# K, V and the first Q tiles from weighted but unnormalised input, with the root mean square applied at the PSUM exit

## The chip, the cores and the metric

The kernel runs as one program on all 8 cores of a Trainium2 chip; each core handles its own tokens and no core waits for another. The metric is device time in microseconds (us) of the slowest core. A program on all eight cores falls into a slower state in some executions: the cores of one die, or of both, show a lower granted TensorE clock (the share of its full speed that the chip allows it), and the run takes some per cent longer.

The engines are named as the profile names them: PE (TensorE), PEld (its weight loads), DVE (VectorE), ACT (ScalarE), POOL (GpSimd) and SP (SyncE, here an issuer of transfers). A `q` after a name (SPq) is the engine's queue, where it issues DMAs.

## The reference

One layer of a decoder: an RMS norm, a wide projection, two branches (sliding-window attention and a gated convolution), gates, and an MLP. Only the first step matters here.

```python
def _rmsnorm(x, g):
    y = x * lax.rsqrt(jnp.mean(x * x, axis=-1, keepdims=True) + EPS)
    return y * g

n = _rmsnorm(hp, norm1_g[l])                 # D_MODEL = 2048
q, k, v, u, g = _project(n, w_in[l], ...)    # one matmul, its columns split
ya = _prompt_attention(q, k, v, sink[l])     # scores, exp, values
# ... u goes through a depthwise convolution of width 31; gates, w_out, MLP follow
```

The root mean square is one number per token, and the projection is linear. So `rmsnorm(x) @ W` equals `(x * g) @ W`, scaled per token afterwards. K, V and Q can therefore be multiplied before the sum of squares is known. The change is built on this.

## The kernel before

Tokens lie on the free axis, features on the 128 partitions in 16 tiles (`XF[...][:, k, :]`). The first group has 768 tokens, processed as three chunks of 256. Each weight "slab" is 2 MB of f32 in DRAM, loaded through GpSimd's queue and converted to bf16 on the way. There are five slots. In the code, `mm` is a chain of matmuls into one PSUM bank, `act` is a ScalarE activation, `tt` and `stt` are VectorE operations on two tensors (`stt` with a per-partition scalar in between), and `P.dma(..., after=[...])` adds a wait for whatever last wrote the tiles that are named.

```python
def first_norm(c):                              # chunk c of the first group
    cc = slice(256 * c, 256 * c + 256)
    pairs = []
    for q in range(4):                          # four quarters of the 16 feature tiles
        t = tI[q]
        act(t[:, :, :], xs[c][:, 4 * q:4 * q + 4, :], AF.Square)
        tt(t[:, 0:2, :], t[:, 0:2, :], t[:, 2:4, :], ALU.add)
        pairs += [(onesf[:, :], t[:, k, :]) for k in range(2)]
    b = bank()
    mm(b[:, 0:256], pairs)                      # 8 f32 matmuls with ones / D
    act(R1[:, cc], b[:, 0:256], AF.Sqrt, bias=EPS)
    P.op("dve", "reciprocal", out=R1[:, cc], in_=R1[:, cc])
    for k in range(16):                         # the 16 scalings
        stt(XF[0][:, k, cc], xs[c][:, k, :], v1(V_G1 + k), R1[:, cc], ALU.mult, ALU.mult)

load_slab(after=[xs[0][:, 0, :]])               # loads are paced: x, slab, x, slab, ...
first_load(1, [wsl[0][:, :]])
load_slab(after=[xs[1][:, 0, :]])
first_load(2, [xs[1][:, 12, :]])
# ... [cut: three more slabs]
first_norm(0)

# ... [cut] in the first group's front:
wk = slab()
keys(wk, 0, 256)                                # K of chunk 0: 2 x 16 matmuls, evicted by ScalarE
first_norm(1)
keys(wk, 256, 256)
wv = slab(load=False)
for t in range(4):
    vals(wv, t)                                 # V of four 128-token tiles
first_norm(2)
load_slab()
keys(wk, 512, 256)
vals(wv, 4)
vals(wv, 5)
load_slab()
constants()
```

`constants` ends with eight products that spread the convolution's taps into small diagonal blocks, and a store of the result to DRAM, from where it is reloaded later in another layout:

```python
for m in range(8):
    P.op("dve", "tensor_tensor", out=cwst[:, m, :, :],
         in0=ctap[:, 32 * m:32 * m + 32].unsqueeze(2).broadcast_to([128, 32, 32]),
         in1=ctap[:, 256:288].unsqueeze(1).broadcast_to([128, 32, 32]), op=ALU.mult)
P.dma("sp", cwb[:, :, :], cwst[...], "d_cwb")
```

After that comes Q (eight tiles of 16 matmuls in each of two column chunks, `128x320` in the trace), and then blocks of attention between the last Q tiles: scores, `exp` into eight probability tiles `PT` (the `exp` also is the PSUM eviction), then the values matmul.

The softmax here doesn't subtract the row's maximum and nothing guards it: scores larger than these inputs give would overflow.

## Time and profile before

| | before |
|---|---|
| time | 3396.55 us median of 3 runs (3395.22 to 3692.71; the highest is a slow run) |
| span of the profiled cores | 3373.6 to 3390.5 us, all fast |
| first K matmul | 19.5 us |
| third chunk's K done | 75.9 us |
| first Q matmul | 79.3 us |
| first scores matmul | 98.9 us |
| first `exp` | 99.5 us |
| first values matmul | 104.4 us |

The last six rows are medians of the eight cores, from the timeline. They serve as milestones throughout.

The page of the kernel before, lines of its parts 1, 2 and 4. Part 2 cuts the span into 40 slices and gives the busy tenths of PE and the granted clock in tenths; part 4 is the chain of work that ended last. In this and all later views, lines in between are left out.

```profile
span 3390.5 us, 59039 instructions; the slowest of 8 cores (3373.6 to 3390.5 us)
PE   6979999999999999999999999999999999999998
PEclk7989999999999999999999999999999999999999
PE 94%; DMA 2%; DVE 2%; SPq 1%; issue 1%; ACT 0%; DVEq 0%; ACTq 0%; POOLq 0%
```

PE is busy 9 tenths or more nearly everywhere. What is left to gain lies in the first slices of about 85 us each, so the most this change could touch is some tens of us in 3390. The start is read from core 1. Its timeline before: start us, duration us, engine, line (one helper records every operation, so all have one line), operation, output<-inputs, shape, count, and in brackets the idle time before it with what ended it.

```profile
18.25 6.42 DVE L157 SCALAR_TENSOR_TENSOR XF_79<-xs_105,vec,R_58 128x256 bf16<-128x256 f32 x16 [0.17 <-DVE R_58 L157]
20.00 8.34 PE L157 MATMUL ps<-XF_79,wsl_49 128*128 128x256 bf16 x32 [4.26 <-DVE XF_79 L157]
66.73 9.38 PE L157 MATMUL ps<-XF_79,wsl_49 128*128 128x256 bf16 x32 [3.17 <-DVE XF_79 L157]
79.44 8.86 PE L157 MATMUL ps<-XF_79,wsl_51 128*128 128x320 bf16 x64
82.71 9.17 DVE L157 TENSOR_TENSOR cwst<-ctap 128x1024 bf16<-128x1024 f32 x8
91.95 0.33 SPq L157 DMA_DIRECT2D cwb<-cwst  x1
99.09 0.61 PE L157 MATMUL ps<-XQ_84,kT 64*128 64x512 bf16 x4
```

Sixteen scalings take 6.42 us, 0.40 us each, and the first sixteen K matmuls of a chunk follow them one by one; the 32 of a chunk take 8.3 to 9.6 us. The Q matmuls in the same list take 0.14 us each, although they are wider. The eight tap products are 1.15 us each on DVE, and the store of their result is issued at 91.95 us.

Where PE waited in the first 110 us of core 1 before (from the waits of PE: total us, times, longest), and its busy time in two stretches (columns: PE, PEld, DVE, ACT and POOL busy, granted clock, DMA share, GB/s):

```profile
PE ps L157 <- DVE tI_101 L157: 12.0, 2, 9.6
PE ps L157 <- DVE XF_79 L157: 10.5, 3, 4.3
PE ps L157 <- ACT tI_102 L157: 2.5, 1, 2.5
```

```profile
0.00:80.00 80.00, 53.41 (x245) 33.91 (x246) 33.41 (x67) 18.95 (x29) 3.50 (x10) 0.81 0.69 151
80.00:110.00 30.00, 30.00 (x222) 20.28 (x219) 13.88 (x14) 10.91 (x23) 6.92 (x12) 1.00 1.01 198
```

The waits are for sums of squares (`tI`) and for scaled input (`XF`). The longest, 9.6 us, is the one from the start of the span to the first sums. The mean clock in the first 80 us reads 0.81. That is too high, since the view counts all time before its first record of the clock as full speed: four matmuls of the sums took 2.05 us at 9.61 us on core 1, and 1.03 us at 14.72 us. The Trainium skill (TensorE: Matmul & The Clock Gate, "Part 1: The HAM clock gate") says that the clock gate passes half the pulses until PE has been busy for some microseconds. The trace agrees in the stretches where scalings pace K: the windows table of core 4 shows a clock of 0.50 from 20 to 25 us and from 40 to 45 us. From 80 to 110 us PE is never idle, at full clock.

### The profile page before, as it was taken

Reading aid. Unit: us, or ns where it says so; the run is one execution under the profiler, and the core shown is the slowest. Engines: PE = TensorE matmul, PEld = TensorE weight load, DVE = VectorE, ACT = ScalarE, POOL = GpSimd, SP = SyncE. Lnnn points to the kernel's source line nnn. Section 1 sums busy time; section 2 is a strip of 40 time slices with the busy share of each in tenths; the row PEclk is TensorE's granted clock in tenths of the full one; section 3 lists DMA queues with packets and bytes.
Section 4 is the critical chain, followed back from the end, with each engine's and each line's share of the span. In section 5 each row is a group of like instructions: output and inputs, shape, how many; then the busy total and the mean of one; then the engine's idle time right before and its main releaser. Section 6 shows DMA issues by size and latency. Waiting matters only on the chain.

```text
span 3390.5 us, 59039 instructions; the slowest of 8 cores (3373.6 to 3390.5 us)
## 1 busy us (share of the span) xinstructions
PE 3312.6 (98%) x22688; PEld 2161.1 (64%) x22688; DVE 1621.9 (48%) x2438; ACT 718.6 (21%) x1371; POOL 267.9 (8%) x475
## 2 busy tenths in 40 slices
PE   6979999999999999999999999999999999999998
PEld 4556776567777775666655666666666666666667
DVE  4534333668889453225288666644542232222225
ACT  2323223321211222112242020203211230101022
POOL 0200000300000000000130000000000000000000
PEclk7989999999999999999999999999999999999999
DMA  6766997467776696858648655555778656668651
GB/s 150 143 119 135 194 188 153 84 123 140 139 142 119 118 197 141 191 110 177 123 83 158 114 102 104 104 102 112 156 165 194 111 110 112 112 109 150 109 106 70
DMA packets 88770, 446.79 MB, mean 132 GB/s; under 512 B 11024, under 2 KB 19920, under 8 KB 45648
## 3 DMA queue, kind: packets, MB, share of 16 engines
q0 software_dynamic: 48240, 349.36, 57.3%
q1 hardware_dynamic: 39968, 93.12, 9.1%
q8 instruction: 187, 3.06, 0.4%
q14 instruction: 87, 0.71, 0.1%
q10 hardware_dynamic: 288, 0.52, 0.0%
HBM read 766.65 MB, written 25.94 MB: 234 GB/s over the span
## 4 chain that ended last, share of the span: by engine, by line
PE 94%; DMA 2%; DVE 2%; SPq 1%; issue 1%; ACT 0%; DVEq 0%; ACTq 0%; POOLq 0%
PE ps L157 94%; SPq L157 1%; DMA ush_89<-um_95 1%; DVE rden_68 L157 0%; DMA wsl_49<-wst 0%; DVE rden_67 L157 0%; DVE H L157 0%; DMA xs_106<-xp 0%; DMA xrP_121<-x 0%; DMA xs_107<-xp 0%; DMA xs_105<-xp 0%; DMA ush_88<-um_94 0%; ACT TQ L157 0%; DVE XF_79 L157 0%; DVE XQ_84 L157 0%
## 5 line engine op out<-in xcount | busy, mean ns | idle before, releaser
L157 DVE TENSOR_TENSOR H<-ps,H 128x320 f32<-128x320 f32 (+4 forms) x400 | 202.7, 507 | 378.1 <-PE ps L157 377.9
L157 PE MATMUL ps<-XF_79,wsl_49 128*128 128x320 bf16 (+3 forms) x1568 | 243.2, 312 | 11.8 <-DVE XF_79 L157 6.3
L157 PE MATMUL ps<-XF_79,wsl_53 128*128 128x320 bf16 (+2 forms) x1472 | 219.6, 309 | 0.0
L157 PE MATMUL ps<-XF_79,wsl_52 128*128 128x320 bf16 (+2 forms) x1472 | 219.4, 310 | 0.0
L157 PE MATMUL ps<-XF_79,wsl_50 128*128 128x320 bf16 (+2 forms) x1472 | 217.7, 308 | 0.8 <-DVE XF_79 L157 0.5
L157 PEld LDWEIGHTS ps<-XF_79,wsl_49 128*128 128x128 bf16 x1568 | 155.1, 99 | 97.0 <-issue 26.4
L157 PE MATMUL ps<-XF_81,wsl_49 128*128 128x384 bf16 (+2 forms) x1344 | 210.2, 317 | 0.0
L157 PE MATMUL ps<-XF_81,wsl_52 128*128 128x384 bf16 (+2 forms) x1344 | 206.0, 314 | 0.0
L157 PE MATMUL ps<-XF_81,wsl_50 128*128 128x384 bf16 (+2 forms) x1280 | 200.0, 317 | 0.0
L157 PE MATMUL ps<-XF_79,wsl_51 128*128 128x320 bf16 (+2 forms) x1344 | 197.8, 307 | 0.0
L157 PE MATMUL ps<-XF_81,wsl_53 128*128 128x384 bf16 (+2 forms) x1280 | 197.4, 315 | 0.0
L157 PEld LDWEIGHTS ps<-XF_79,wsl_53 128*128 128x128 bf16 x1472 | 143.5, 98 | 73.0 <-issue 2.7
L157 PEld LDWEIGHTS ps<-XF_79,wsl_52 128*128 128x128 bf16 x1472 | 143.7, 98 | 72.1 <-issue 1.4
L157 PEld LDWEIGHTS ps<-XF_79,wsl_50 128*128 128x128 bf16 x1472 | 143.4, 98 | 71.7 <-issue 4.0
L157 PE MATMUL ps<-XF_81,wsl_51 128*128 128x384 bf16 (+2 forms) x1216 | 186.5, 314 | 0.0
L157 PEld LDWEIGHTS ps<-XF_81,wsl_49 128*128 128x128 bf16 x1344 | 132.0, 98 | 74.6 <-issue 0.4
L157 DVE SCALAR_TENSOR_TENSOR tAP<-tAP,ps 128x384 f32<-128x384 f32 (+1 forms) x64 | 34.4, 537 | 302.5 <-PE ps L157 301.6
L157 PE MATMUL ps<-XF_80,wsl_49 128*128 128x352 bf16 (+4 forms) x1184 | 178.8, 311 | 0.0
L157 PEld LDWEIGHTS ps<-XF_81,wsl_52 128*128 128x128 bf16 x1344 | 131.3, 98 | 71.3 <-issue 1.0
L157 PEld LDWEIGHTS ps<-XF_79,wsl_51 128*128 128x128 bf16 x1344 | 131.1, 98 | 63.7 <-issue 2.1
L157 PEld LDWEIGHTS ps<-XF_81,wsl_50 128*128 128x128 bf16 x1280 | 125.6, 98 | 71.3 <-issue 1.4
L157 PE MATMUL ps<-XF_80,wsl_51 128*128 128x352 bf16 (+4 forms) x1120 | 170.6, 313 | 0.0
(406 smaller groups left out, 4575.5 us busy)
## 6 DMA issues: line engine op xcount, KB each, us to landing
wsl_49<-wst POOLq DMA_DIRECT2D x66, 1024.0 KB, 8.2
wsl_50<-wst POOLq DMA_DIRECT2D x66, 1024.0 KB, 8.3
wsl_51<-wst POOLq DMA_DIRECT2D x65, 1024.0 KB, 8.3
wsl_52<-wst POOLq DMA_DIRECT2D x65, 1024.0 KB, 8.2
wsl_53<-wst POOLq DMA_DIRECT2D x65, 1024.0 KB, 8.1
xrP_121<-x SPq DMA_DIRECT2D x18, 384.0 KB, 7.6
xrP_123<-x SPq DMA_DIRECT2D x18, 352.0 KB, 5.4
H<-x SPq DMA_DIRECT2D x16, 384.0 KB, 10.2
```

The source lines that it names most:

```text
L157: i = getattr(eng, ins[0])(**ins[1])
```

## The change

Its intent: K, V and four Q tiles (two of the eight in the code's count, each in two column chunks) read `x * g`, which needs no root mean square; the results are scaled as they leave PSUM, where an eviction is needed anyway. The squares are added on GpSimd, which has nothing to do at that time, and PE sums four tiles instead of eight. All of x is loaded at once, without pacing. The tap products move to GpSimd and into the memory of the probability tiles, because their old place is now the weighted input's.

```diff
-        cwst = over(X[1], 0, "cwst", [128, 8, 32, 32], BF16)
-        ctap = over(X[1], 16384, "ctap", [128, 288], F32)
+        cwst = over(PT[0], 0, "cwst", [128, 8, 32, 32], BF16)
+        ctap = over(X[2], 16384, "ctap", [128, 288], F32)
# ... [cut]
+        P.dma("act", vec[:, :], vecs[:, :], "d_vec")
+        for c in range(3):
+            first_load(c)                       # no after=
+        def squares(c, q):
+            t = tI[q]
+            act(t[:, :, :], xs[c][:, 4 * q:4 * q + 4, :], AF.Square)
+            for k in (2, 1):
+                P.op("pool", "tensor_tensor", out=t[:, 0:k, :], in0=t[:, 0:k, :], in1=t[:, k:2 * k, :], op=ALU.add)
+        def weigh(c, q):                        # XF[1] = x * g, one op of 128x1024 per quarter
+            ...
+        def first_rstd(c):
+            mm(b[:, 0:256], [(onesf[:, :], tI[q][:, 0, :]) for q in range(4)])
+            ...                                 # Sqrt, reciprocal as before
# ... [cut] constants():
-                P.op("dve", "tensor_tensor", out=cwst[:, m, :, :],
+                P.op("pool", "tensor_tensor", out=cwst[:, m, :, :],
# ... [cut] front of the first group:
+                first_keys(0)                   # evicted by VectorE, times R1
+                for q in range(4):
+                    first_scale(0, q)           # 4 of the old 16 scalings, for the later projections
+                    squares(1, q)
+                    weigh(1, q)
+                first_rstd(1)
+                first_keys(1)
+                for t in range(4):
+                    first_vals(t)               # evicted by ScalarE with a per-token scale
+                for q in range(4):
+                    first_scale(1, q)
+                    squares(2, q)
+                    weigh(2, q)
+                    if q < 2:
+                        load_slab(after=[xs[2][:, 4 + 8 * q, :]])
+                first_rstd(2)
+                first_keys(2)
+                first_vals(4)
+                first_vals(5)
+                load_slab()
+                load_slab()
+                for q in range(4):
+                    first_scale(2, q)
+                constants()
# ... [cut] Q:
-                    b = fm(w, j % 2, nT, halo + c0, n)
-                    act(qo[:, j, c0:c0 + n], b[:, 0:n], AF.Copy)
+                    b = fm(w, j % 2, XF[1] if first and j < 2 else nT, halo + c0, n)
+                    if first and j < 2:
+                        tt(qo[:, j, c0:c0 + n], b[:, 0:n], R1[:, halo + c0:halo + c0 + n], ALU.mult)
+                    else:
+                        act(qo[:, j, c0:c0 + n], b[:, 0:n], AF.Copy)
```

The third Q tile and everything after it still read scaled input, so the 48 scalings remain; they only move later.

More of the change, by code (lines that the diff above doesn't have):

```diff
@@ L359, in drain, with first_load @@
                 side.pop(0)()
-        for q in range(4):
-            P.dma("sp", xs[0][:, 4 * q:4 * q + 4, :], xp[0][:, 4 * q:4 * q + 4, :], f"d_x{q}")
-        P.dma("sp", vec[:, :], vecs[:, :], "d_vec")
+        def first_load(c):
+            for q in range(4):
+                P.dma("sp", xs[c][:, 4 * q:4 * q + 4, :], xp[c][:, 4 * q:4 * q + 4, :], f"d_x{q}")
+        P.dma("act", vec[:, :], vecs[:, :], "d_vec")
+        for c in range(3):
+            first_load(c)
         P.dma("sp", ctap[:, :], cwd[:, :], "d_ct")
@@ L383, in add_square @@
                 tt(dst[:, c0:c0 + n], dst[:, c0:c0 + n], t, ALU.add)
-        def first_norm(c):
-            cc = slice(256 * c, 256 * c + 256)
-            pairs = []
-            for q in range(4):
-                t = tI[q]
-                act(t[:, :, :], xs[c][:, 4 * q:4 * q + 4, :], AF.Square)
-                tt(t[:, 0:2, :], t[:, 0:2, :], t[:, 2:4, :], ALU.add)
-                pairs += [(onesf[:, :], t[:, k, :]) for k in range(2)]
+        one = S1[0:1, 0:1]
+        P.op("dve", "memset", ap=one, constant=1.0)
@@ new lines, in squares @@
+        def squares(c, q):
[4 more added lines that the diff above has]
+        def weigh(c, q):
+            f = slice(4 * q, 4 * q + 4)
+            P.op("dve", "tensor_tensor", out=XF[1][:, f, 256 * c:256 * c + 256], in0=xs[c][:, f, :],
+                 in1=vec[:, V_G1 + 4 * q:V_G1 + 4 * q + 4].unsqueeze(2).broadcast_to([128, 4, 256]), op=ALU.mult)
@@ L394, in first_norm, with first_scale @@
+        def first_rstd(c):
+            cc = slice(256 * c, 256 * c + 256)
             b = bank()
-            mm(b[:, 0:256], pairs)
+            mm(b[:, 0:256], [(onesf[:, :], tI[q][:, 0, :]) for q in range(4)])
             act(R1[:, cc], b[:, 0:256], AF.Sqrt, bias=EPS)
             P.op("dve", "reciprocal", out=R1[:, cc], in_=R1[:, cc])
-            for k in range(16):
+        def first_scale(c, q):
+            cc = slice(256 * c, 256 * c + 256)
+            for k in range(4 * q, 4 * q + 4):
@@ L399, in first_norm @@
                 stt(XF[0][:, k, cc], xs[c][:, k, :], v1(V_G1 + k), R1[:, cc], ALU.mult, ALU.mult)
-        def first_load(c, after):
-            for q in range(4):
-                P.dma("sp", xs[c][:, 4 * q:4 * q + 4, :], xp[c][:, 4 * q:4 * q + 4, :], f"d_x{q}", after=after)
-        load_slab(after=[xs[0][:, 0, :]])
-        first_load(1, [wsl[0][:, :]])
-        load_slab(after=[xs[1][:, 0, :]])
-        first_load(2, [xs[1][:, 12, :]])
-        load_slab(after=[xs[2][:, 0, :]])
-        load_slab()
@@ L411, in build, with first_column @@
-        first_norm(0)
+        def first_column(t):
+            b = bank()
+            mm(b[:, 0:1], [(R1[0:1, 128 * t:128 * t + 128], one)])
+            act(S2[:, t:t + 1], b[:, 0:1], AF.Copy)
+        load_slab()
+        for q in range(4):
+            squares(0, q)
+            weigh(0, q)
+        load_slab(after=[xs[1][:, 4, :]])
+        first_rstd(0)
         def constants():
@@ L652, in front, with first_keys, first_vals @@
             if first:
-                wk = slab()
-                keys(wk, 0, 256)
-                first_norm(1)
-                keys(wk, 256, 256)
-                wv = slab(load=False)
-                for t in range(4):
-                    vals(wv, t)
-                first_norm(2)
+                wk, wv = slab(), slab(load=False)
+                def first_keys(c):
+                    cc = slice(256 * c, 256 * c + 256)
+                    for a in range(2):
+                        b = fm(wk, a, XF[1], 256 * c, 256)
+                        tt(kT[:, a, cc], b[:, 0:256], R1[:, cc], ALU.mult)
+                def first_vals(t):
+                    first_column(t)
+                    b = bank()
+                    mm(b[:, 0:256], [(XF[1][:, k, 128 * t:128 * t + 128], wv[:, k, :]) for k in range(16)])
+                    act(vtok[:, t, :], b[:, 0:256], AF.Copy, scale=S2[:, t:t + 1])
+                first_keys(0)
[5 more added lines that the diff above has]
+                first_keys(1)
+                for t in range(4):
+                    first_vals(t)
+                for q in range(4):
+                    first_scale(1, q)
[7 more added lines that the diff above has]
+                first_vals(5)
                 load_slab()
-                keys(wk, 512, 256)
-                vals(wv, 4)
-                vals(wv, 5)
                 load_slab()
+                for q in range(4):
+                    first_scale(2, q)
                 constants()
```

## The prediction

> **What bounds it now.** TensorE: the page shows PE busy 98% of a 3390.5 us span, and its own work is 94% of the chain of waits. Only the start differs, PE 6 of 10 in the first of 40 slices. By the timeline the Q projection starts at 80.24 us, while K and V before it are 96 + 96 matmuls that need about 0.11 us each warm, some 21 us. The rest is: the first x chunk (7.1 to 13.3 us), sums of squares through PE (8 fp32 matmuls per chunk), a 1.75 us reciprocal, and three times 16 scalings of 0.40 us on DVE which pace K matmuls at 0.40 us each with the granted clock at 0.5 (8.6, 9.6 and 9.4 us for 32 matmuls).
>
> **What the change does to the start.** K, V and four Q tiles read weighted x, ready without the reciprocal. fp32 sums are halved on PE, but GpSimd adds come into the chain: the Trainium skill (GPSIMD Engine Reference, section 3.1) has 4497 ns for a 2048-wide two-input fp32 add, so I estimate 1.2 + 0.6 us per quarter against 0.69 on DVE. x and the first slab now share the DMA engines from the start (about 6.5 us per chunk, 7 per slab by the windows table), so x lands near 16.5 instead of 13.3 us and K starts near 20.5 us as before, ending near 26.5 (before 29.1). Per chunk DVE has 6.4 us of scalings and an estimated 4.6 us of weighing. In the third chunk ACT squares wait in order behind the V evictions, and GpSimd adds compete with DVE there (the skill, SBUF — State Buffer, "Who interferes with whom": a DVE instruction with two SBUF inputs contends with GpSimd reads), so PE idles about 10 us before the third K. I expect the third K to end near 66 and Q to start near 70 us: 9 to 10 us gained.
>
> **Where I think it is given back.** The convolution weights now are built on GpSimd, in the memory of the probability tiles. GpSimd starts them only after the fifth slab issue, which waits for the third K (66 us). Eight products cost DVE 1.15 us each; on GpSimd I estimate 2.2 to 3 us (same section; the one 512-wide one-input op in the trace takes 1.49), 18 to 24 us, plus some blocking by the last scalings. Then the store to DRAM (16.6 us before, again beside slabs) must land before any exp may write its tile: near 106 us, estimated. Before, the first exp ran at 100.45. ACT, in order, then holds Q evictions, and PE stops at the second score group, two Q tiles ahead: idle from about 92 to 106 us; the first values matmul, at 105.4 before, comes at about 109. Downstream all keeps its order.
>
> **Sum:** -10 at Q, +14 at the exp: +3 us net, 3400 us; range 3385 to 3413. A size over 2% (68 us) isn't in the start at all: faster 0.01, same 0.98, slower 0.01.
>
> **What would show it.** Q projection's first matmul near 70 us; PE idle ahead of the third K, released by GpSimd adds; GpSimd products of 2 to 3 us each from about 67 us; first exp released by the store of the weights at about 106 us and not by PE; values matmuls within 5 us of before.
>
> **What would make it wrong.** GpSimd products near 1.5 us, or a store of 10 us: then the exp is free by 95 us and the change gains 5 to 10 us. Products of 4 us or scalings starved by GpSimd would lose 10 to 15 us.

## The result, and the profile after

| | before | after |
|---|---|---|
| runs of the same rounds | 3692.71 (slow), 3395.22, 3396.55, 3396.97 | 3473.65, 4021.21, 3451.89 (all slow), 3400.25; besides: 3396.05, 3396.16 (fast) |
| ratio of fast runs | | 1.0004 (0.9981 to 1.0026) |
| the changed kernel run again, five fast runs | | 1.003 (1.0005 to 1.0055), 3404.97 to 3425.66 us |

A ratio here is the mean time of one kernel's fast runs over that of the other's fast runs of the same rounds, so it is not quite the ratio of the medians quoted. The record has two more fast runs of the first comparison, and its ratio of 1.0004 is what the three give: a mean of 3397.5 us against 3396.2 us. The 0.3% of the second comparison is about 10 us. Both results lie within 2%.

The rounds ran on different chips, and the fast runs of the kernel before had means of 3393.7, 3398.4 to 3401.2 and 3407.9 us there. Ratios compare the same rounds only. The milestones of the kernel before come from one profile, of a run of 3392.01 us.

The cores view of the kernel after, with each die's median:

```profile
die 0 (median of its cores): 3390.6 us, clock 0.990
die 1 (median of its cores): 3446.3 us, clock 0.969
```

So cores 0 to 3 are read. Their median span, 3390.6 us, compares with 3383.1 us for the same four cores before.

| milestone, us | before | after | difference |
|---|---|---|---|
| first K matmul | 19.5 | 25.1 | +5.6 |
| third chunk's K done | 75.9 | 76.6 | +0.7 |
| first Q matmul | 79.3 | 80.7 | +1.4 |
| first scores matmul | 98.9 | 107.3 | +8.4 |
| first `exp` | 99.5 | 107.9 | +8.4 |
| first values matmul | 104.4 | 112.8 | +8.4 |

In the fast profile of the second run, on eight cores, the same row of six reads 25.3, 76.7, 80.8, 107.4, 108.0 and 112.9 us, so the slow die has not bent these numbers.

The start of core 1 after, by the timeline (as above; buffer numbers are left out in this profile):

```profile
17.66 1.06 ACT L157 ACTIVATE tI<-xs 128x1024 f32<-128x1024 f32 x1 [5.47 <-DMA xs<-xp]
18.86 5.02 POOL L157 TENSOR_TENSOR tI<-tI 128x512 f32<-128x512 f32 x4 [4.20 <-ACT tI L157]
25.01 4.60 PE L157 MATMUL ps<-XF,wsl 128*128 128x256 bf16 x32
57.42 3.88 ACT L157 ACTIVATE tI<-xs 128x1024 f32<-128x1024 f32 x4
58.61 3.10 POOL L157 TENSOR_TENSOR tI<-tI 128x512 f32<-128x512 f32 x2 [22.17 <-ACT tI L157]
61.97 1.19 PE L157 MATMUL ps<-tI,onesf 128*128 128x256 f32 x2 [5.02 <-POOL tI L157]
70.27 5.83 PE L157 MATMUL ps<-XF,wsl 128*128 128x256 bf16 x32
76.55 15.93 DVE L157 SCALAR_TENSOR_TENSOR XF<-xs,vec,R 128x256 bf16<-128x256 f32 x2
92.26 0.33 SPq L157 DMA_DIRECT2D cwb<-cwst  x1
92.62 14.23 PE L157 MATMUL ps<-XF,wsl 128*128 128x320 bf16 x63 [1.20 <-DVE XF L157]
105.77 0.32 SPq L157 DMA_DIRECT2D cw<-cwb  x1
106.78 0.61 PE L157 MATMUL ps<-XQ,kT 64*128 64x512 bf16 x4
107.38 1.26 ACT L157 ACTIVATE PT<-ps,vec 128x512 bf16<-128x512 f32 x2
```

A longer window of the same view groups the products into one row:

```profile
77.19 15.00 POOL L157 TENSOR_TENSOR cwst<-ctap 128x1024 bf16<-128x1024 f32 x8
```

A window of DVE from 77.1 to 92.3 us holds one instruction only:

```profile
76.94 15.54 DVE L157 SCALAR_TENSOR_TENSOR XF<-xs,vec,R 128x256 bf16<-128x256 f32 x1
```

The waits of PE in the first 110 us of core 1 after, and its two stretches:

```profile
PE ps L157 <- POOL tI L157: 34.1, 11, 11.9
PE ps L157 <- DVE XF L157: 5.2, 4, 1.7
```

```profile
0.00:80.00 80.00, 41.92 (x226) 27.90 (x227) 42.85 (x58) 17.82 (x28) 33.17 (x36) 0.83 0.66 144
80.00:110.00 30.00, 28.10 (x172) 17.02 (x171) 20.65 (x25) 6.40 (x13) 15.59 (x14) 0.89 0.87 171
```

Three things are to be seen.

1. K of the first and the third chunk did get faster: 32 matmuls in 4.60 and 5.83 us, against 8.34 and 9.38 us. K of the second did not: it ran from 37.57 to 48.31 us, in four pieces that wait for weighings behind scalings on DVE (39.16 to 48.72 us before). PE is busy 11.5 us less in the first 80 us (41.92 against 53.41), for nearly the same projections and half as many sums.
2. None of it arrived at Q. PE's waits for the sums of squares, which now come from GpSimd, grew to 34.1 us (14.5 us before, for `tI` from DVE and ScalarE); the longest, 11.9 us, is again the one from the start of the span. K of a chunk doesn't need the sums, but it stands behind their matmuls in PE's order. Ahead of the third K the ones-matmuls run from 61.97 to about 70 us at the pace of the GpSimd additions, and those could only begin when ScalarE reached the squares, at 57.42 us.
3. A new loss came up after Q had begun. Two scalings took 15.93 us, in the very time in which GpSimd ran its eight products (77.19 to 92.19 us). The second of the two alone took 15.54 us, and ended 0.29 us after the last product. The Q matmuls that read scaled input then ran on the last scalings' heels, the second group at 92.62 us, and PE took 26.6 us from the first Q matmul to the first scores, against 19.6 us before (medians).

The ledger of the medians closes: +1.4 us at Q, +7.0 us between Q and scores, 0.0 us from scores to values (5.5 us in both), together +8.4 us at the first values matmul.

### The profile page after: what moved, and what is told of

The parts are those of the page before. It is cut to its first block, busy times and chain, and to the rows that moved or that the text cites. A ratio compares the mean times of both kernels' runs of the same rounds, so it can differ in the third digit from the quotient of the medians.

```text
span 3450.1 us, 59066 instructions; the slowest of 8 cores (3387.9 to 3450.1 us)
## 1 busy us (share of the span) xinstructions
PE 3379.8 (98%) x22676; PEld 2183.0 (63%) x22676; DVE 1642.8 (48%) x2441; ACT 715.9 (21%) x1367; POOL 308.0 (9%) x507
## 4 chain that ended last, share of the span: by engine, by line
PE 92%; DVE 3%; DMA 2%; issue 1%; ACT 1%; POOL 0%; SPq 0%; DVEq 0%; ACTq 0%; POOLq 0%
PE ps L157 92%; DMA wsl<-wst 1%; DVE XF L157 1%; DMA xrP<-x 1%; DVE H L157 1%; DMA xs<-xp 0%; DVE rden L157 0%; POOL tI L157 0%; ACT TQ L157 0%; SPq L157 0%; DVE S L157 0%; DMA ush<-um 0%; DVE wpr L157 0%; DVE XQ L157 0%; DVE LR L157 0%
## 5 line engine op out<-in xcount | busy, mean ns | idle before, releaser
L157 PE MATMUL ps<-XF,wsl 128*128 128x384 bf16 (+4 forms) x19392 | 2953.8, 316 | 7.5 <-DVE XF L157 5.3
L157 PEld LDWEIGHTS ps<-XF,wsl 128*128 128x128 bf16 x19392 | 1912.0, 99 | 1046.5 <-issue 33.8
L157 DVE SCALAR_TENSOR_TENSOR acc<-XU,vec,acc 128x768 f32<-128x768 bf16 (+1 forms) x480 | 439.7, 945 | 1.1 <-ACT acc L157 1.1
L157 POOL DMA_DIRECT2D wsl<-wst x327 | 173.7, 531 | 2855.0 <-PE ps L157 2832.5
L157 ACT ACTIVATE XF<-rt 128x320 bf16<-128x320 f32 (+2 forms) x384 | 189.7, 496 | 1132.6 <-DVE rt L157 1132.3
L157 DVE SCALAR_TENSOR_TENSOR rt<-ps,LM 128x320 f32<-128x320 f32 (+2 forms) x384 | 199.9, 523 | 403.3 <-PE ps L157 400.0
L157 DVE TENSOR_TENSOR S<-S,TQ 128x320 f32<-128x320 f32 (+4 forms) x164 | 91.2, 556 | 127.0 <-ACT TQ L157 127.0
L157 PE MATMUL ps<-XU,wsl 128*128 128x320 bf16 (+2 forms) x768 | 129.8, 326 | 0.0
L157 PE MATMUL ps<-XQ,wsl 128*128 128x320 bf16 (+2 forms) x768 | 129.8, 326 | 0.0
L157 DVE RECIPROCAL rden<-rden 128x512 f32<-128x512 f32 (+1 forms) x36 | 114.3, 3174 | 3.7
L157 PEld LDWEIGHTS ps<-XQ,wsl 128*128 128x128 bf16 x768 | 77.9, 101 | 43.9
L157 PEld LDWEIGHTS ps<-XU,wsl 128*128 128x128 bf16 x768 | 77.9, 101 | 43.9
L157 POOL TENSOR_SCALAR_AFFINE_SELECT PT<-PT 128x512 bf16<-128x512 bf16 x128 | 77.9, 640 | 120.5 <-ACT PT L157 120.4
```

Source lines behind the costliest of these rows:

```text
L157: i = getattr(eng, ins[0])(**ins[1])
```

## The experiments

Three questions were open after this reading, each with rivals. **Why is Q late?** Because the third chunk's squares stand behind the V evictions on ScalarE (order); or because GpSimd adds slowly and holds DVE up (adder); or because x and slabs now share the DMA engines (loads). **Why does it take 7 us more to the scores?** Because GpSimd's products starve the scalings; or because Q's evictions moved. **Does the store hold the first `exp`,** as predicted, or is it merely late by chance? The texts were written ahead of each run; where they use a letter for a theory, the numbers beside it say which of these is meant. Every run below gave correct results. Milestones are medians of eight cores, and of cores 0 to 3 for `e2_products_dve`, whose profile was slow on one die.

| run | K | Q | last scaling | scores | `exp` | values | ratio to before (95%) |
|---|---|---|---|---|---|---|---|
| before | 19.5 | 79.3 | 72.2 | 98.9 | 99.5 | 104.4 | 1 |
| after, run again | 25.3 | 80.8 | 98.6 | 107.4 | 108.0 | 112.9 | 1.003 (1.0005 to 1.0055) |
| e1_adds_dve | 23.3 | 83.6 | 101.4 | 110.0 | 110.6 | 115.5 | 1.005 (1.0027 to 1.0072) |
| e2_products_dve | 25.3 | 81.1 | 83.9 | 100.8 | 113.2 | 115.2 | 1.0037 (1.0008 to 1.0066) |
| e3_squares_early | 25.3 | 73.7 | 91.5 | 99.6 | 100.2 | 105.2 | 1.0024 (0.9961 to 1.0086) |
| e4_paced_loads | 20.9 | 79.2 | 96.9 | 105.5 | 106.1 | 111.1 | 1.0037 (1.0009 to 1.0066) |
| e5_sums_on_pe | 21.6 | 60.7 | 78.4 | 87.0 | 87.6 | 92.6 | 0.9964 (0.9943 to 0.9985) |
| e6_products_act | 41.2 | 92.7 | 95.4 | 112.4 | 112.9 | 117.9 | 1.0025 (1.0002 to 1.0048) |
| e7_weigh_first | 41.4 | 92.8 | 110.4 | 118.8 | 119.3 | 124.3 | 1.0044 (1.0025 to 1.0064) |
| e8_products_early | 27.6 | 83.7 | 86.4 | 103.4 | 103.9 | 108.9 | 0.9983 (0.9964 to 1.0001) |
| e9_sums_pe_products_early | 26.1 | 65.8 | 68.5 | 85.4 | 85.9 | 90.9 | 0.9955 (0.9932 to 0.9978) |
| e10_weigh_first | 25.4 | 58.2 | 67.2 | 77.9 | 78.4 | 83.4 | 0.9915 (0.990 to 0.993) |
| e12_slab_unheld | 22.0 | 59.8 | 68.8 | 79.4 | 80.0 | 84.9 | 0.9965 (0.9933 to 0.9997) |

The first four each undo or move one thing in the changed kernel.

### e1_adds_dve: the additions back on VectorE

```diff
-                P.op("pool", "tensor_tensor", out=t[:, 0:k, :], in0=t[:, 0:k, :], in1=t[:, k:2 * k, :], op=ALU.add)
+                tt(t[:, 0:k, :], t[:, 0:k, :], t[:, k:2 * k, :], ALU.add)
```

> Changed kernel with the square sums added on VectorE again (0.69 + 0.42 us a quarter) instead of GpSimd. Theory A (the wait before the third K is one of order: ScalarE squares the third chunk only behind the V evictions, at 57 us, whoever adds): VectorE now waits for those squares itself and weighs behind them, so the third K ends no earlier than in the changed kernel (76 us), rather 80, and the Q projection starts at 80 to 85 us. Rival B (the slow GpSimd adds, 2.1 to 3.1 us a quarter, set the start): the third K ends near 66 and Q starts near 70 us. Time: A 3398 to 3405, B 3388 us.

Q came later, at 83.6 us instead of 80.8 us, although the first K came 2 us earlier. The timeline of core 1 says why:

```profile
58.59 3.88 ACT L157 ACTIVATE tI<-xs 128x1024 f32<-128x1024 f32 x4
59.74 1.22 DVE L157 TENSOR_TENSOR tI<-tI 128x512 f32<-128x512 f32 x2 [8.20 <-ACT tI L157]
```

A faster adder (1.22 us for the two additions of a quarter, against 2.1 to 3.1 us on GpSimd) didn't help, because it too waits for ScalarE's squares, 8.20 us of idle DVE, and DVE then also holds back its weighing behind them. In the third chunk the speed of the adder isn't the cause; the squares' place in ScalarE's order comes first. (The run is no clean test of the adder's speed, since it loads the engine that weighs; e5 takes the additions away.)

### e2_products_dve: the tap products back on VectorE, after the scalings

```diff
-                P.op("pool", "tensor_tensor", out=cwst[:, m, :, :],
+                P.op("dve", "tensor_tensor", out=cwst[:, m, :, :],
```

> Changed kernel with the eight products for the convolution weights on VectorE again, behind the scalings. Theory C (the GpSimd products hold the SBUF reads that the scalings need, so 16 scalings take 21.5 us and the Q projection waits for them): the scalings take 6.5 us and the first scores come at about 100 instead of 107 us; the Q start stays at 80. But the products end at about 93 us and the store lands at 107 to 109, so the first exp is then released by the store, at about 108 us as now, and the time stays within 3 us of the changed kernel's. Rival D (the Q tiles are slow for another reason, the granted clock or full PSUM banks): first scores stay at 106 to 108 us.

Core 1, by the timeline:

```profile
77.00 6.42 DVE L157 SCALAR_TENSOR_TENSOR XF<-xs,vec,R 128x256 bf16<-128x256 f32 x16
86.39 9.17 DVE L157 TENSOR_TENSOR cwst<-ctap 128x1024 bf16<-128x1024 f32 x8
95.63 0.33 SPq L157 DMA_DIRECT2D cwb<-cwst  x1
100.37 0.61 PE L157 MATMUL ps<-XQ,kT 64*128 64x512 bf16 x4
111.72 1.26 ACT L157 ACTIVATE PT<-ps,vec 128x512 bf16<-128x512 f32 x2 [10.75 <-DMA cwb<-cwst]
```

Sixteen scalings take 6.42 us again, and from Q to scores it is 19.7 us again (81.1 to 100.8): the starvation is gone, and with it the 7 us. Q's evictions were left as the change has them, so they aren't the cause. But now ScalarE idles 10.75 us ahead of the first `exp` until the store has landed, because the products lie in the probability tiles that the `exp` overwrites, and values come at 115.2 us, later than in the changed kernel. So the predicted store mechanism exists. In the changed kernel the starved scalings hide it: there the store landed at 105.8 us (SP issues the reload that waits for it at 105.77), 1 us before PE's scores at 106.78 us.

### e3_squares_early: the third chunk's squares ahead of the V evictions on ScalarE

```diff
                 first_keys(1)
+                for q in range(4):
+                    squares(2, q)
                 for t in range(4):
                     first_vals(t)
                 for q in range(4):
                     first_scale(1, q)
-                    squares(2, q)
                     weigh(2, q)
```

> Changed kernel with one move: the squares of the third chunk (ScalarE) and their adds (GpSimd) are issued before the V tiles instead of behind them. Theory A (order on ScalarE): the third K follows the fourth V tile without a wait, from 57 us, K ends near 61 and Q starts near 65 us instead of 80. Products then run from about 62 to 77 us, the starved scalings end near 82, first scores near 91, the store lands near 92 and the first exp comes at about 92 to 93 us (107 in the changed kernel). Time about 13 us less than the changed kernel's, near 3385. Rival B (GpSimd adds are the limit): Q starts no earlier than 75 us.

Q began at 73.7 us, 7.1 us earlier than with the changed kernel. That is the share of the order: of the squares on ScalarE, and with them of the additions on GpSimd. I had expected some 65 us; the additions on GpSimd now ran beside VectorE's weighing and scaling and held those up, and the second chunk's K ended near 55 us instead of 48 us. The time did not move outside its interval, which is wide here (four fast runs that differ by 26 us). The starvation simply came earlier. Core 1:

```profile
69.65 21.45 DVE L157 SCALAR_TENSOR_TENSOR XF<-xs,vec,R 128x256 bf16<-128x256 f32 x16
70.28 14.99 POOL L157 TENSOR_TENSOR cwst<-ctap 128x1024 bf16<-128x1024 f32 x8
```

Sixteen scalings in 21.45 us beside GpSimd's products, in another time window and with other neighbours than before: the blocking goes with the products.

### e4_paced_loads: x loads paced as in the kernel before

```diff
-        for c in range(3):
-            first_load(c)
+        first_load(0)
...
-        load_slab()
+        load_slab(after=[xs[0][:, 0, :]])
+        first_load(1, [wsl[0][:, :]])
+        first_load(2, [xs[1][:, 12, :]])
```

> Changed kernel with the x loads and the first slab paced as in the kernel before (first slab after the first quarter of x, second chunk after the slab, third after the second). Theory E (unpaced loads cost the first K 4 to 5 us, by sharing the DMA engines, and pay it back in the second chunk): the first K starts near 21 instead of 25 us, the second chunk comes later, and Q starts within 3 us of 80. Rival F (the unpaced loads are what eats the gain): Q starts at 75 us or earlier.

Pacing gives back 4.4 us at the first K (20.9 against 25.3 us), but only 1.6 us at Q and 1.8 us at values. The unpaced loads explain hardly anything further on. Nor do they explain the late first K alone: e5 below keeps them, drops the additions, and has its first K at 21.6 us. It takes both to delay it.

### e5_sums_on_pe: no additions at all

Squares are written in bf16 and summed by 16 bf16 matmuls with ones in each chunk; the squares have room for all three chunks and stand early in ScalarE's order as in e3. (bf16 squares are a looser way to sum.)

```diff
-        tI = [over(X[2], i * 4096, f"tI{i}", [128, 4, 256], F32) for i in range(4)]
+        tI = [over(X[2], i * 2048, f"tI{i}", [128, 4, 256], BF16) for i in range(12)]
...
-            for k in (2, 1):
-                P.op("pool", "tensor_tensor", out=t[:, 0:k, :], ...)
...
-            mm(b[:, 0:256], [(onesf[:, :], tI[q][:, 0, :]) for q in range(4)])
-            act(R1[:, cc], b[:, 0:256], AF.Sqrt, bias=EPS)
+            mm(b[:, 0:256], [(onesb[:, :], tI[4 * c + q][:, k, :]) for q in range(4) for k in range(4)])
+            act(R1[:, cc], b[:, 0:256], AF.Sqrt, scale=1.0 / D, bias=EPS)
```

> The kernel of the early squares with the GpSimd adds taken away altogether: ScalarE writes the squares in bf16 and 16 bf16 matmuls with ones sum them, so GpSimd does nothing but issue slabs until its eight products. Theory G (GpSimd adds still cost the start, by waits of PE and by holding the SBUF reads of VectorE's two-input instructions): first K near 21 us (25), VectorE's scalings and weighings of the second chunk take 11 to 12 us (14.5 in the changed kernel), Q starts near 58 us (73 with the early squares alone). Rival: the adds are hidden, and Q stays at 68 or later. The products starve the last scalings as before (about 21 us), so first scores come about 27 us after Q starts, near 86 us, and the time is about 3382 us.

Q begins at 60.7 us, 20 us before the changed kernel's and 13 us before e3's. So the additions, through their own time and through what they do to VectorE, cost 13 us, and ScalarE's order 7 us. The 13 us include what the smaller bf16 squares and their own buffers bring; no run separates these. This version is 0.36% faster than the kernel before, even though the 16 scalings are still starved: from Q to scores 26.3 us.

### e6_products_act and e7_weigh_first: the products on ScalarE

The idea of e6 was to take the products off both GpSimd and VectorE: 32 ScalarE copies with a per-partition scale, each writing every 32nd column of `cwst`. e7 also weighs the next chunk before the last is scaled.

```diff
+        def products(q):
+            for c in range(8 * q, 8 * q + 8):
+                act(cwst[:, :, :, c].rearrange("p m t -> p (m t)"), ctap[:, 0:256], AF.Copy, scale=ctap[:, 256 + c:257 + c])
```

> As the run before, with the products for the convolution weights on ScalarE (32 activations with the unit column as scale, 0.4 us each, in its idle time of the first 30 us), and their store issued once the third x chunk has landed: GpSimd does no arithmetic before the attention. Theory C: the last 16 scalings take 6.5 us, first scores follow 20 us after the Q start (26 to 27 in the changed kernel), near 78 us, and the first exp is released by the scores, as the store lands near 50 us. Time 3370 to 3378. Rival D: scores still come 26 us after the Q start.

> As the run before, with VectorE's order turned: the weighing of the next chunk ahead of the scaling of the last, so K and V of every chunk wait for x and nothing else of VectorE; all scalings run beside V and the first Q tiles. If the order on VectorE is what holds the second and third K, Q starts near 50 us, first scores near 70, and the time is 3364 to 3370, 0.8% below the kernel before. If the DMA engines are the limit by then (three chunks, six slabs, one store: about 69 us of transfers), the Q tiles wait for slabs and first scores come at 75 to 80 us.

Both missed. I had expected these copies to take about what an ordinary 128x256 activation takes in this trace, 0.38 us. Group of the tile `cwst` in e6 on core 0 (lowest, median and highest ns of one):

```profile
L157 ACT ACTIVATE cwst<-ctap x32: 1386/1405/1419, 13.6 to 64.2; 128x256 bf16<-128x256 f32 x32
```

They took 1.405 us, with outputs 64 bytes apart, and the squares stood behind them: the first K came at 41.2 us. The Trainium skill (SBUF — State Buffer, the note on cachelines in "Door 1: The DMA port swizzle") says that an access that crosses into a new 16-byte line pays a penalty; the direction agrees, and no run here isolates that as the cause. Two facts can still be taken from e6: with no products on GpSimd, from Q to scores it is 19.7 us and the last 16 scalings end 2.7 us after Q's start, in 6.41 us. That confirms starvation by the products from a third side. e7 can't say what weighing first is worth, since the same miss masks it; e10 asks again. Its 25.9 us from Q to scores are not starvation: all 48 scalings stood behind the late squares there, and ran undisturbed (on core 1 16 in 6.42 us and 32 in 12.75 us, 89.91 to 109.67 us). VectorE that is merely late delays Q as much as one that is blocked; it is the 15.54 us of one instruction that tells the two apart.

### e8_products_early: the changed kernel, with the products on VectorE in its idle first 20 us

The taps are loaded first, the eight products are spread through the time in which VectorE waits for x, and the store goes out when x's third chunk has landed.

```diff
+        P.dma("act", ctap[:, :], cwd[:, :], "d_ct")
         P.dma("act", vec[:, :], vecs[:, :], "d_vec")
...
-        load_slab()
+        load_slab(after=[ctap[:, :], vec[:, :]])
+        products(0, 3)
         for q in range(4):
             squares(0, q)
             weigh(0, q)
+            if q < 2:
+                products(3 + 2 * q, 5 + 3 * q)
+        P.dma("sp", cwb[:, :, :], cwst[...], "d_cwb", after=[xs[2][:, 12, :]])
```

> Changed kernel with one thing moved: the eight products run on VectorE (1.2 us each) in its idle time of the first 18 us, their input loaded first and the first slab held until it has landed; their store is issued when the third x chunk has landed. Adds and order of squares stay as in the changed kernel. Where the products at the old place on VectorE (second run) freed the scores at 100 us but left the first exp at 112 to 115, released by the store, the store now lands near 50 us: so if the store alone held the exp, the first exp follows the first scores at 100 us and the first values matmul comes at 105 instead of 113 to 117. Rival: something else holds ScalarE, and the exp stays later than 108. Q start 78 to 81 us. Time 3391 to 3397, as the kernel before.

Core 1 by the timeline:

```profile
11.47 14.69 POOL L157 TENSOR_TENSOR tI<-tI 128x512 f32<-128x512 f32 x8
83.23 19.72 PE L157 MATMUL ps<-XF,wsl 128*128 128x320 bf16 x144
102.89 0.61 PE L157 MATMUL ps<-XQ,kT 64*128 64x512 bf16 x4
103.43 1.27 ACT L157 ACTIVATE PT<-ps,vec 128x512 bf16<-128x512 f32 x2
```

The 144 Q matmuls run without a gap in 19.72 us, and the `exp` follows the scores by 0.5 us. Both second-half losses are gone: starvation and store. What stays is Q at 83.7 us (expected 78 to 81), because the sums are as in the changed kernel, and those of the first chunk became slower: beside the products on VectorE GpSimd took 14.69 us for the four quarters' additions, against 9.56 us in the changed kernel, and the first K, at 27.6 us, followed the sums at once. The time is 0.17% below the kernel before, with an interval that just reaches 1, while its values matmul is 4.5 us later than before. This is the one run in which time and milestones point in different directions. The kernel before was not profiled on that chip, where it took 3407.9 us; I leave it open.

### e9_sums_pe_products_early: e5 and e8 together

> All three repairs together: squares of the third chunk early, summed by TensorE in bf16 without adds, products on VectorE in its idle time of the first 18 us. If the three causes add up, Q starts near 60 us as with the sums on TensorE, the last scalings take 6.5 us instead of 21, first scores come 20 us after Q starts, near 80 us, first values near 85 us, and the time is 3370 to 3377 (19 us less at the values than the kernel before). If the products delay the weighing of the first chunk, Q starts at 63 to 66 us.

Q at 65.8 us, scores 19.6 us later, values at 90.9 us: 13.5 us before the kernel before. The time is 0.45% lower, a mean of 3390.6 us against 3407.9 us. The parts add up as expected except that Q is 5 us later than in e5, because the first K comes at 26.1 instead of 21.6 us. I had put that down to the products, which push the first weighing back. The trace names the first slab, which this run holds back until the taps have landed, as in e8; so on all eight cores (8.7 to 11.0 us), and on core 1 the weighing was done at 22.9 us:

```profile
26.53 6.00 PE L157 MATMUL ps<-XF,wsl 128*128 128x256 bf16 x32 [10.12 <-DMA wsl<-wst]
```

### e10_weigh_first: and weigh the next chunk before the last is scaled

K and V of a chunk need only the weighing. The scalings are needed from the third Q tile on. So the scalings of chunks 0 and 1 move behind the weighing of the next chunk, or behind K of the last. (Not shown: `constants` moves ahead of the third K, with its last four copies behind the scalings; and the V tiles are issued behind the weighing of the third chunk.)

```diff
                 for q in range(4):
-                    first_scale(0, q)
                     squares(1, q)
                     weigh(1, q)
...
-                for q in range(4):
-                    first_scale(1, q)
                     weigh(2, q)
...
                 for t in range(4):
                     first_vals(t)
+                for q in range(4):
+                    first_scale(0, q)
                 first_rstd(2)
...
                 for q in range(4):
+                    first_scale(1, q)
+                for q in range(4):
                     first_scale(2, q)
```

> As the run before, with VectorE's order turned: each next chunk is weighed before the last is scaled. If VectorE's order holds the second and third K, Q starts near 50 us, first scores near 70 to 72, first values near 76, and the time is 3362 to 3370. If the DMA engines limit by then (three chunks, six slabs and a store need about 69 us), PE waits for slabs and first scores come at 75 us or later.

This is the fastest version: 0.9915 (0.990 to 0.993), five fast runs from 3377.01 to 3381.61 us against a mean of 3407.9 us in the same rounds, 29 us less. It beats both kernels. Core 1 by the timeline, and its first 80 us in the windows view:

```profile
7.11 3.50 DVE L157 TENSOR_TENSOR cwst<-ctap 128x1024 bf16<-128x1024 f32 x3 [5.64 <-DMA ctap<-cwd]
24.82 6.45 PE L157 MATMUL ps<-XF,wsl 128*128 128x256 bf16 x32 [9.24 <-DMA wsl<-wst]
49.05 3.66 PE L157 MATMUL ps<-XF,wsl 128*128 128x256 bf16 x32
53.16 12.75 DVE L157 SCALAR_TENSOR_TENSOR XF<-xs,vec,R 128x256 bf16<-128x256 f32 x32
56.86 19.72 PE L157 MATMUL ps<-XF,wsl 128*128 128x320 bf16 x144
76.52 0.60 PE L157 MATMUL ps<-XQ,kT 64*128 64x512 bf16 x4
```

```profile
0.00:80.00 80.00, 57.22 (x422) 42.30 (x423) 52.01 (x90) 25.16 (x41) 7.18 (x17) 1.00 0.96 205
```

Thirty-two scalings run under the first Q matmuls in 12.75 us, undisturbed at 0.40 us each; GpSimd was busy for 7.18 us in all; and the DMA share rose from 0.69 to 0.96, probably because slab slots come free earlier. The clock column reads 1.00, but it has no record before 30.6 us, and the first K ran slower: 32 matmuls in 6.45 us, against 3.66 us for those at 49.05 us. The table counts 422 matmuls of PE in those 80 us against 245 before (48 of them for the sums in both).

The first case that I expected (Q near 50, scores at 70 to 72 us) was missed: they came at 58.2 and 77.9 us. The second, that PE waits for slabs, holds for the first slab only. From 40 to 80 us PE was busy for 40.00 us on every core. What is left to gain at the start lies before that: on core 1 PE worked for 17.22 of the first 40 us.

### e11_changed_again: the changed kernel itself

> The changed kernel itself once more, because only one of its four timed runs fell in the fast state. If its later first values matmul (8 us) reaches the end of the program, its fast runs are 5 to 10 us above the kernel before (ratio 1.0015 to 1.003); if the shifting transfers of the convolution absorb it, the ratio lies within 0.999 and 1.001. Milestones within 2 us of the first profile: Q at 80 to 82, scores at 106 to 109.

Five fast runs, 3404.97 to 3425.66 us, and a ratio of 1.003 (1.0005 to 1.0055). The first result, 1.0004 from three fast runs, lies just below this interval, and its own interval (0.9981 to 1.0026) overlaps it. One run weighs heavily: without 3425.66 us, the other four are 5.5 us above the fast runs before (3406.7 against 3401.2 us). The milestones say +8.4 us, +0.3% is about 10 us, and the first result is 1.2 us. So the change gained nothing and cost something between 1 and 10 us; that it cost anything is shown by the second comparison only.

### e12_slab_unheld: e10 without holding the first slab back for the taps

The taps are also loaded behind the table of vectors again, and their store is issued after the last five products.

```diff
-        load_slab(after=[ctap[:, :], vec[:, :]])
-        products(0, 3)
+        load_slab()
...
+            if q == 1:
+                products(0, 3)
...
                 first_keys(0)
+                products(3, 8)
```

> The best version so far with the first slab issued at once again, instead of held until the two small tables had landed (which took until 13 us and put its landing at 25 to 28 us), and the products split: three between the weighings of the first chunk, five behind the first K. If the held slab is what kept the first K at 25 to 28 us, it starts at 21 to 23, the first scores come at 72 to 75 instead of 77 to 79, and the time falls by 2 to 5 us more. If VectorE is the limit (its scalings ended 0.2 us ahead of their first reader in the best version), scores stay at 77 to 79.

The first K came 3.4 us earlier (22.0 us), but the five products that then stood behind it delayed the second chunk's weighing, and Q was 1.6 us later than in e10. Scores, at 79.4 us, came as in the expectation's second case. The time, 0.9965 (0.9933 to 0.9997), spreads over 26 us. It is not better than e10, and e10's wait of 9.24 us for its first slab, seen above, is not simply there to be had.

### From the first values matmul to the whole time

Ordered by their first values matmul, most runs line up: 83.4 us, −0.85% (e10); 90.9 us, −0.45% (e9); 92.6 us, −0.36% (e5); 104.4 us, 0 (before); 105.2 us, +0.24% with a wide interval (e3); 111.1 us, +0.37% (e4); 112.9 us, +0.3% (e11); 115.2 us, +0.37% (e2); 115.5 us, +0.5% (e1). A gain at the start mostly survives to the end. Not all do: e12 (84.9 us, −0.35%) gains less than its start, e6 and e7 (117.9 and 124.3 us, +0.25% and +0.44%) lose less than theirs, and e8 has been named. What blurs it is the stage after: the convolution is fed by DMAs which shift rows, and there the end of the last convolution matmul scatters between the cores of a single run, 247.6 to 271.0 us before and 255.7 to 266.4 us in e11. In e10 it was 224.8 to 237.6 us. From that end to the end of the span, cores took 3119 to 3133 us before and 3123 to 3144 us in e10, so no gain is to be seen later. More can't be said, since the two profiles come from different rounds: the fast runs of the kernel before took 3396.2 us in the mean in the one and 3407.9 us in the other.

## Why the prediction was right or wrong, point by point

- **What bounds the kernel, and how much could be won.** Right. PE is busy 98% of the span, and both results lie within 2% of before. Even the best recombination moved the time by 0.85%.
- **First K near 20.5 us, as before.** Wrong by 4.6 us: 25.1 us. (The prediction's times are those of core 4, some 1 us behind the medians: first K 20.5 against 19.5 us before.) The last quarters of chunk 0 landed at about 17.7 us on core 1 (predicted 16.5), and the additions of a quarter took 2.2 to 2.5 us of GpSimd (predicted 1.8), two quarters one after the other: 18.86 to 23.88 us. e4 shows that pacing the loads again is worth 4.4 us here, and e5 that dropping the additions is worth 3.7 us with the loads unpaced.
- **Third K ends near 66, Q near 70 us, 9 to 10 us gained.** This is the step that failed: 76.6 and 80.7 us, nothing gained. The mechanism was named (squares behind the V evictions, GpSimd additions, contention with VectorE, PE idle ahead of the third K and released by GpSimd), and the trace shows it. Its sizes were too small. e3 measures the order on ScalarE at 7 us and e5 the additions, with what they do to VectorE (and with the bf16 squares, not separated), at another 13 us. In the second chunk, VectorE took 14.4 us on core 1 for its scalings and weighing (30.05 to 44.4 us), where I had 11.0 us without blocking.
- **GpSimd products of 2.2 to 3 us each, 18 to 24 us.** The trace has 1.88 us each, 15.0 us in all. I had scaled a figure of the Trainium skill (GPSIMD Engine Reference, section 3.1: 4497 ns for a two-input f32 addition of 2048 elements per partition) by the element count, which gives 2.25 us. Here the output is bf16 and the inputs are broadcast.
- **"Plus some blocking by the last scalings".** The wrong way round, and mis-sized. The products did not slow; the scalings stopped. The skill (SBUF — State Buffer, "Who interferes with whom") says that a VectorE instruction with two SBUF inputs contends with a GpSimd instruction that reads SBUF. The trace agrees: a scaling that takes 0.40 us alone took 15.54 us. The sum had nothing for this; it measured 7.0 us between Q and scores (e2, e6 and e8 take it away, each by another way). The text had listed "scalings starved by GpSimd would lose 10 to 15 us" under what would make it wrong. The starvation is what happened; the loss at the values matmul was 8.4 us.
- **First `exp` held by the store, near 106 us.** The number was nearly right by cancelling errors: products started at 77.2 us instead of 67, took 15.0 instead of about 21 us, and the store took 13.5 us (92.26 to 105.77) instead of 16.6. The releaser was wrong: PE, not the store, since the scores were late as well, at 106.78 us. e2 shows that the store does hold the `exp` as soon as the scores are on time.
- **Values matmuls within 5 us of before (109 us).** Wrong: +8.4 us, 112.8 us.
- **The sum, +3 us net, 3400 us.** The fast runs of the same rounds gave 3396.05 to 3400.25 us, 1.2 us over before in the mean. The second measurement, +0.3%, puts the loss nearer 10 us. The sum's two terms were −10 at Q and +14 afterwards; they measured +1.4 and +7.0. The time was met with both terms off, in opposite directions. That is luck, and it proves little: the range of 3385 to 3413 us also holds the time before, 3396.55 us.

Still open: why one scaling had to wait through several GpSimd instructions and wasn't let in between them (the trace shows the durations, not the hand-over); why e8 isn't slower although its values matmul is 4.5 us later; and how much of e10's gain at the convolution comes from earlier slabs rather than from earlier values.

## What to carry to other kernels

Taking a value off the critical path gains nothing while the work that makes it still stands ahead, in order, on the engine that should run free: here K didn't need the sums, but stood behind their matmuls on PE, and those behind squares on ScalarE. Before moving work to an idle engine, ask which busy engine shares its way to memory in that very time: 15 us of "free" GpSimd work stopped VectorE for as long. Work without early inputs belongs into the idle start, and operations that a later consumer needs belong behind those that the next one needs; these two, with sums on PE, turned a loss of at most about 0.3% into a gain of 0.85%.

## What the Trainium skill lacked or had wrong

- **SBUF — State Buffer, "Who interferes with whom".** The rule held. What the page lacks is how long it may last: it speaks of the shared ports being held for an instruction. Here VectorE finished only two scalings in 15.93 us while GpSimd ran eight products back to back, each 1.88 us long. The wait spanned the whole sequence and didn't end with one instruction, although by the records the stalled scaling had started first (76.94 us, the first product 77.19 us).
- **GPSIMD Engine Reference, section 3.1.** Its figures for two-input elementwise work (4497 ns, about 2.6 cycles an element) are for f32 at 2048 elements per partition. A 1024-wide product with broadcast f32 inputs and a bf16 output took 1.88 us on GpSimd and 1.15 us on VectorE, a ratio of 1.6 where the page has 1.96. The additions of a quarter (512 and then 256 elements, f32) took 2.1 to 2.2 us with little or no work of VectorE beside them, 3.1 us beside its weighing, and some 3.7 us beside its products (e8).
- **No page has a figure for ScalarE writes with a stride.** A 128x256 copy with a scale, bf16 outputs 64 bytes apart, took 1.405 us, against 0.47 us for an eviction from PSUM of the same size, with a scale too, to contiguous addresses (`vtok`). The cacheline note of the SBUF page fits the direction only.
- **DMA: Bandwidth & Descriptors, "Queues, rings and completion order".** The page says that an engine goes round between its queues packet by packet. What that means for a small transfer has no number: the 144 KB table of taps, issued at the start on its own queue, was waited for until 14.0 us on core 1 and 14.9 us on core 0, beside x and the first slab (e7), and until 7.1 us on core 1 when it was issued first on its queue and the slab was held back until it had landed (e10).
